# Seven gather buffers instead of eight, and a fourth kept unit of query weights, in a four-layer decoder trunk

## The chip, the core and the metric

The kernel runs on one core of a Trainium2 chip. The metric is the device time of one execution in microseconds (us); lower is better. Three executions of the kernel before took 3229.98, 3231.82 and 3232.85 us, so their median is 3231.82 us.

The core has five engines with instruction streams of their own: TensorE (PE, matrix products, with a separate weight load, PEld), VectorE (DVE), ScalarE (ACT), GpSimd (POOL) and SyncE (SP). They meet through semaphores. Sixteen DMA engines move data from device memory into the on-chip memory. Here POOL starts the gathers, and SP starts the plain loads of weights.

## The reference

The reference is a decoder trunk for one sequence of 256 tokens of width 1024, in float32. It has four layers. Each layer adds a token mixer and then a feed-forward part to the residual stream:

```python
for i in range(DEPTH):                       # DEPTH = 4
    h = h + mixer[i % 3](rmsnorm(h, norm_mix[i]), ...)      # HGRN2, FoX, Mamba-2 SSD, HGRN2
    h = h + peer_ffn(rmsnorm(h, norm_ffn[i]), peer_w_q[i], peer_keys[i], peer_u[i], peer_v[i])
return rmsnorm(h, norm_final)
```

The feed-forward part (PEER) is what fills the time. Each token forms 8 queries from a weight matrix of 1024 x 2048, scores two lists of 128 keys a query, keeps the best 16 of the 256 sums, and so names 16 experts a query. An expert is one row of `u` and one row of `v`, 1024 numbers each, out of a table of 16384 experts a layer:

```python
q = (xb @ w_q).reshape(M, 8, 2, 128)
...                                          # two top-16 lists, their sums, top 16 again: idx, gates
u, v = u_tab[idx], v_tab[idx]                # 128 experts of a token, 8 KB each
act = gelu(einsum('md,mhkd->mhk', xb, u)) * gates
return einsum('mhk,mhkd->md', act, v)
```

So 256 tokens x 128 experts x 4 layers x 8 KB have to come from device memory, beside the weights of the mixers and of the queries.

## The kernel before

**Stages.** The 256 tokens are two tiles of 128. A layer and a tile make a stage, eight in all (`STAGES`), in the order layer 0 tile 0, layer 0 tile 1, layer 1 tile 0, and so on. The main loop of a stage takes its 64 pairs of gathers. Beside them, as "side work", it runs the mixer, the normalisation and the queries of the *next* stage (`side`, `ready`, `queries`), so that the experts of the next stage are known when this one ends. The eighth stage has almost no side work. The loop spreads the side work by costs that are written out by hand (`SIDE`, `SPAN`, `products_`, `others`).

**Gathers.** One gather brings 128 rows of 8 KB, a `u` row and a `v` row together, into one buffer of 128 x 2048 numbers (1 MB): two experts of 64 tokens, as the token's number decides the partition. Two gathers are a pair, which serves two experts of all 128 tokens, so there are 512 pairs and 1024 gathers. The buffers `GB[0]` to `GB[NGB - 1]` form a ring, and gather n goes to buffer n modulo NGB. `fetches(i)`, called at the start of pair i, hands POOL all gathers below 2i + NGB whose experts are known. The work on a pair is in `dot` and `spread`. DVE multiplies the `u` half with the token (in place) and sums it up, one instruction a gather. ACT applies the activation and the gate, and spreads the result on a diagonal (`dg`). PE multiplies that with the `v` half into two accumulators (`acc`, L1257); four float32 products a pair are eight records in the profile. When the last of them is done the two buffers are free, and POOL, which waits for that (L1221), issues the next two gathers.

**Weights.** All weights come in units of 1 MB, in a fixed sequence (`stream`): the units of a layer's mixer, then its eight query units `wq`, for tile 0 and again for tile 1. `loads()` issues them from SP (L303) in the order of `order`, as long as a place is free. A unit's place is one of three:

- one of the `NRAW` = 3 rotating `raw` buffers, given free when PE has used the unit
- a place named in `homes`, only in the first stage, where the gather buffers and the mixer's memory still lie idle; these units need no `raw` buffer
- for the first `NKEPT` units of a layer's `wq`, a place in `kept`. It is loaded for tile 0 and not again for tile 1 of the same layer; such a unit needs no `raw` buffer either

`loads()` is called each time PE has used up a unit (`half`). Of the eight `wq` units of a layer, three are kept, so tile 1 loads five.

**Memory.** `kept`, the ring `gb` and the rest lie side by side in one tile, `arena`; a unit and a gather buffer have the same size.

**The end.** After the last gather, PE has to wait for DVE and ACT before the last pair's products. `warm` issues products on constants into a spare bank, with no use for their result; in the last pair there is one of them ahead of the products (L1239, float32, two records). Then the last normalisation runs on DVE and ACT, and the result is written.

Of the kernel before, what the change touches and what calls it, by code (L numbers as in the profile page):

```python
# [25 lines left out]
HALF = UNIT // 2  # L26
TOPK = 16
NQ = TOPK // 2
NGB = 8
NRAW = 3  # L30
MIX = 10464
STAGES = 2 * DEPTH
NKEPT = 3

FREE = {"hg": 0, "fox": 64 + 8 * T + 2 * D, "ssd": 352 + 4 * D + 96}
SPACE = 7 * D + P
# [128 lines left out]
def trunk(ctx: ExitStack, tc: tile.TileContext, d: dict, out: bass.AP):  # L165
# [12 lines left out]
    cst = cpool.tile([P, ncst], F32, name="cst")  # L178
    par = cpool.tile([P, npar], F32, name="par")
    fst = cpool.tile([P, P + 8 * 2 * DEPTH], F32, name="fst")  # L180
    sizes = (("h", 2 * D), ("xT", D), ("XR", 2 * D), ("keys", UNIT), ("SS", 2048), ("mix", MIX), ("kept", NKEPT * UNIT),
             ("gb", NGB * 2 * D))
    arena = cpool.tile([P, sum(n for _, n in sizes)], F32, name="arena")
# [8 lines left out]
    SS = at_["SS"].rearrange("p (h c k) -> p h c k", h=8, c=2)  # L192
    GB = [at_["gb"][:, i * 2 * D:(i + 1) * 2 * D] for i in range(NGB)]
    mix = at_["mix"]
# [17 lines left out]
    def act(o, i, f, **k):  # L212

        if f not in ghosts:
            table[0] = f
        nc.scalar.activation(o, i, f, **k)  # L216
# [36 lines left out]
    def bank():  # L253
        return psp.tile([P, 512], F32, name="ps")
# [7 lines left out]
            stream += [(nm, i) for i in range(UNITS[KIND[l] if KIND[l] != "ssd" else "ssm"])]  # L262
            stream += [("wq%d" % l, i) for i in range(8)]

    homes = {3: GB[0], 4: GB[1], 17: GB[0], 18: GB[1], 19: GB[2], 23: GB[5], 24: GB[6]}
    homes.update({28 + i: mix[:, o:o + UNIT] for i, o in enumerate((SPACE, D, 3 * D))})
    order = [0, 1, 2, "rest", *range(3, 9), 23, 9, 10, 11, 24, 12, 13, 14, 22, 15, 16, "x", 17, 20, 18, 21, 19, "keys",
             "factors", 28, 25, "heads", 29, 26, 27, "states", 30]
# [7 lines left out]
    def loads():  # L276

        while order:
# [11 lines left out]
            else:  # L290
                nm, i = stream[u]
                keep = nm[0] == "w" and i < NKEPT
                if keep:
# [925 lines left out]
    def fetch(n):  # L1219
        (s, hh, q), g = pairs[n // 2], n % 2  # L1220
        nc.gpsimd.indirect_dma_start(GB[n % NGB], None, d["uv"],  # L1221
                                     bass.IndirectOffsetOnAxis(ap=got[s, hh][0][:, g, q:q + 1], axis=0))

    def fetches(n):

        while sent[0] < 2 * len(pairs) and sent[0] < 2 * n + NGB and pairs[sent[0] // 2][:2] in got:
            fetch(sent[0])
            sent[0] += 1

    def dot(i, g):  # L1230
        if g == 0:
            acts[i] = wk2.tile([P, 3, 2], F32, name="dots", bufs=4)
        u = GB[(2 * i + g) % NGB][:, 0:D]
        stt(u, u, 1.0, XR[:, g], op0=OP.mult, op1=OP.mult, accum_out=acts[i][:, 0, g:g + 1])

    def warm(n, b, x):

        for _ in range(n):
            nc.tensor.matmul(b, x[:, 0:P], x[:, 0:512], start=True, stop=True)  # L1239

    def spread(i):
        s, hh, q = pairs[i]
        a = acts.pop(i)
        dg = wk2.tile([P, 2, 64], F32, name="dg", bufs=4)
        act(a[:, 1], a[:, 0], AF.Gelu)
        for g in range(2):
            act(a[:, 2, g:g + 1], a[:, 1, g:g + 1], AF.Copy, scale=got[s, hh][1][:, g, 1, q:q + 1])
        for g in range(2):
            act(dg[:, g], m64, AF.Copy, scale=a[:, 2, g:g + 1])
        if hh == 0 and q == 0:  # L1250
            accs[s] = [accp.tile([P, 512], F32, name="acc") for _ in range(2)]
        if i == len(pairs) - 1:
            warm(1, bank(), cst)
        for e in range(2):
            for g in range(2):
                v = GB[(2 * i + g) % NGB][:, D + e * 512:D + (e + 1) * 512]
                nc.tensor.matmul(accs[s][e][g * 64:g * 64 + 64], dg[:, g], v, start=hh == 0 and q == 0,  # L1257
                                 stop=hh == 7 and q == NQ - 1)
# [67 lines left out]
    for s in range(STAGES):  # L1326
# [23 lines left out]
        for i in range(64 * s, 64 * s + 64):  # L1350
            new, end = i % 64 == 0 and s > 0, i % 64 == 63 and s + 1 < STAGES
            fetches(i)
            dot(i, 0)
            if end:
                for o, b in x[:2]:
                    nc.scalar.copy(o, b)
            elif new:

                products_(True)
                others()  # L1360
            dot(i, 1)
            spread(i)
            if end:
                (_, b), (o, c) = x[2:]
                nc.scalar.copy(x[2][0], b)
                vec.tensor_copy(o, c)
            route_steps(3, i // 8 + 3)
            others()
            products_()
            if i % 64 == 62 and s + 1 < STAGES:  # L1370
                while not state["done"]:
                    others()
                    products_(True)
                others()
                x = repeated()
            if table[0] is not AF.Gelu:
                act(spare, eps, AF.Gelu)
# [20 lines left out]
```

## Time and profile before

| what | value |
|---|---|
| median of three executions | 3231.82 us |
| time of the profiled execution | 3228.44 us |
| its span, first to last instruction | 3225.7 us |
| PE busy | 2490.0 us (77%) |
| DVE busy | 2117.9 us (66%) |
| ACT busy | 1352.9 us (42%) |
| POOL busy | 1182.8 us (37%) |
| moved by DMA | 1322.99 MB, mean 410 GB/s |

The profiled execution is 3.4 us below the median of the others. Its span leaves out 2.7 us that lie around it. In the views, a group is named by its line, engine and tile (`arena<-in_uv,ix` is a gather into the ring, `acc<-arena,dg` a product of `v` rows). A wait is put down to the instruction or the DMA that ended last. A line of the timeline begins with the start in us and the length in us. In a table of stretches the last three columns are the granted TensorE clock as a share of full speed, the mean busy share of the 16 DMA engines and what they moved in GB/s; a share can read 1.01 since packets overlap a little.

### The profile page before, as it was taken

What the parts mean: (1) busy time and instruction counts of PE and PEld (TensorE: products, weight loads), DVE (VectorE), ACT (ScalarE), POOL (GpSimd) and SP (SyncE); (2) the same over time, 40 slices, a digit from 0 to 9 for tenths busy, and PEclk for the clock granted to TensorE, in tenths of its full rate; (3) what the DMA queues carried; (4) which work ended last, traced back from release to release, by engine and by line L of the source; (5) the groups of instructions that cost most, each with busy time, mean ns of one, the idle gap of its engine ahead of it and who ended that gap; (6) DMA issues with size and microseconds to landing.
All of it is one profiled execution on the core that took longest, in us unless ns stands there. A gap on an engine that the chain in (4) does not pass through costs nothing.

```text
span 3225.7 us, 30835 instructions
## 1 busy us (share of the span) xinstructions
PE 2490.0 (77%) x8606; PEld 1102.5 (34%) x8606; DVE 2117.9 (66%) x5584; ACT 1352.9 (42%) x3895; POOL 1182.8 (37%) x1030
## 2 busy tenths in 40 slices
PE   9888787777777886898778897878777788866565
PEld 4433233233333432344233443333323333332222
DVE  2476657566666866788567876576666667667764
ACT  3353334253334633477234673354433544333332
POOL 0243334333443443333334333343433343334443
PEclk9999898888899897999889998889988998888777
DMA  7899999999999999999999999999999999999997
GB/s 312 345 421 421 421 421 419 420 412 410 421 418 421 399 421 414 420 421 419 412 416 418 416 420 409 416 413 421 418 418 416 409 421 420 413 413 416 419 417 329
DMA packets 182761, 1322.99 MB, mean 410 GB/s; under 512 B 20289, under 2 KB 20673, under 8 KB 21825
## 3 DMA queue, kind: packets, MB, share of 16 engines
q0 software_dynamic: 147456, 1073.81, 80.6%
q1 hardware_dynamic: 35136, 247.23, 18.6%
q8 instruction: 71, 1.16, 0.1%
q14 instruction: 98, 0.79, 0.1%
HBM read 1319.90 MB, written 1.05 MB: 410 GB/s over the span
## 4 chain that ended last, share of the span: by engine, by line
DMA 56%; PE 18%; DVE 9%; issue 8%; ACT 5%; POOL 3%; POOLq 0%; SPq 0%; DVEq 0%; ACTq 0%
DMA arena<-in_uv,ix 56%; PE acc L1257 9%; DVE arena L203 7%; PE pj L238 6%; POOL arena L1221 3%; PE ps L238 3%; ACT dots L216 2%; ACT L216 1%; ACT dg L216 1%; PE ps L242 1%; ACT arena L216 1%; DVE si L203 0%; DVE eq L203 0%; DMA raw<-in_ssm 0%; DVE sv L203 0%
## 5 line engine op out<-in xcount | busy, mean ns | idle before, releaser
L1221 POOL DMA_INDIRECT arena<-in_uv,ix x1024 | 1180.7, 1153 | 2017.0 <-PE acc L1257 1475.8
L203 DVE SCALAR_TENSOR_TENSOR arena<-arena 128x1024 f32<-128x1024 f32 (+3 forms) x1282 | 1322.1, 1048 | 907.3 <-DMA arena<-in_uv,ix 848.5
L1257 PE MATMUL acc<-arena,dg 128*64 128x512 f32 x4096 | 1306.0, 723 | 712.8 <-ACT dg L216 697.9
L1257 PEld LDWEIGHTS acc<-arena,dg 128*64 128x64 f32 x4096 | 474.9, 154 | 1354.9 <-ACT dg L216 1021.5
L238 PE MATMUL pj<-raw,arena 128*128 128x512 f32 x1648 | 772.5, 611 | 3.7 <-DMA raw<-in_ssm 1.6
L216 ACT ACTIVATE dots<-dots 128x2 f32<-128x2 f32 x512 | 103.6, 202 | 1531.6 <-DVE arena L203 1529.2
L238 PEld LDWEIGHTS pj<-raw,arena 128*128 128x128 f32 x1648 | 301.4, 193 | 482.2 <-issue 470.6
L216 ACT ACT_TABLE_LOAD x325 | 417.0, 1283 | 6.8 <-DVE arena L203 0.8
L216 ACT ACTIVATE dg<-m,dots 128x64 f32<-128x64 f32 x1024 | 292.5, 333 | 0.0
L216 ACT ACTIVATE dots<-dots,gs 128x1 f32<-128x1 f32 x1024 | 245.6, 286 | 16.7
L238 PE MATMUL ps<-arena 128*128 128x128 f32 (+3 forms) x992 | 130.2, 288 | 1.3 <-ACT arena L1087 0.9
L238 PEld LDWEIGHTS ps<-arena 128*128 128x128 f32 (+2 forms) x992 | 103.0, 168 | 67.8 <-issue 43.2
L238 PE MATMUL pj<-arena 128*128 128x512 f32 (+1 forms) x288 | 125.8, 584 | 0.3 <-DVE arena L203 0.3
L242 PEld LDWEIGHTS ps<-fst,arena 128*128 128x128 f32 x568 | 68.5, 148 | 88.9 <-issue 42.7
L242 PE MATMUL ps<-fst,arena 128*128 128x128 f32 x568 | 92.8, 291 | 7.7 <-DVE arena L203 5.0
L216 ACT ACTIVATE arena<-arena 128x512 f32<-128x512 f32 (+3 forms) x132 | 67.7, 554 | 43.3 <-DVE arena L203 40.9
L203 DVE DVE_READ_ACCUMULATOR arena<-arena 128x1 f32 x1024 | 83.9, 82 | 0.0
L238 PEld LDWEIGHTS pj<-arena 128*128 128x128 f32 x288 | 53.0, 192 | 71.4 <-issue 61.7
L203 DVE FIND_INDEX8 si<-sv,arena 128x8 uint32<-128x128 f32 x256 | 69.8, 284 | 0.0
L203 DVE MAX8 sv<-arena 128x8 f32<-128x128 f32 x256 | 61.7, 282 | 10.3 <-ACT arena L1091 5.7
L238 PE MATMUL ps<-cst,arena 128*128 128x128 f32 (+3 forms) x288 | 68.0, 364 | 0.0
L203 DVE COPY gs<-ig 64x16 f32<-64x16 f32 (+1 forms) x256 | 51.8, 202 | 4.7
(116 smaller groups left out, 1232.6 us busy)
## 6 DMA issues: line engine op xcount, KB each, us to landing
raw<-in_hg SPq DMA_DIRECT2D x72, 1024.0 KB
raw<-in_ssm SPq DMA_DIRECT2D x64, 1024.0 KB
raw<-in_wq SPq DMA_DIRECT2D x38, 1024.0 KB
raw<-in_fox SPq DMA_DIRECT2D x32, 1024.0 KB
arena<-in_uv,ix POOLq DMA_INDIRECT x1024
arena<-in_wq SPq DMA_DIRECT2D x14, 1024.0 KB
arena<-in_hg SPq DMA_DIRECT2D x8, 1024.0 KB
arena<-in_keys SPq DMA_DIRECT2D x4, 1024.0 KB
```

The source lines that it names most:

```text
L203: return getattr(nc.vector, name)(o, *a, **k)
L216: nc.scalar.activation(o, i, f, **k)
L238: nc.tensor.matmul(o, w, m, start=start, stop=stop)
L242: nc.tensor.transpose(o, i, ident)
L1221: nc.gpsimd.indirect_dma_start(GB[n % NGB], None, d["uv"], bass.IndirectOffsetOnAxis(ap=got[s, hh][0][:, g, q:q + 1], axis=0))
L1257: nc.tensor.matmul(accs[s][e][g * 64:g * 64 + 64], dg[:, g], v, start=hh == 0 and q == 0, stop=hh == 7 and q == NQ - 1)
```

## The change

The ring has seven buffers. Its eighth megabyte goes to `kept`, which now holds four units: the units 0 to 3 of each layer's `wq` are loaded for tile 0 and stay for tile 1. The size of `arena` stays the same, and all buffers of the ring begin one place further on.

In the first stage, unit 23 of the stream (the fourth query unit of layer 0) was loaded to `GB[5]` and unit 24 to `GB[6]`. Unit 23 now goes to its place in `kept`, and unit 24 to `GB[5]`. The order of the loads is unchanged.

In the last pair, `warm` issues two products on constants instead of one.

```diff
-NGB = 8
+NGB = 7
...
-NKEPT = 3
+NKEPT = 4
...
-    homes = {3: GB[0], 4: GB[1], 17: GB[0], 18: GB[1], 19: GB[2], 23: GB[5], 24: GB[6]}
+    homes = {3: GB[0], 4: GB[1], 17: GB[0], 18: GB[1], 19: GB[2], 24: GB[5]}
...
         if i == len(pairs) - 1:
-            warm(1, bank(), cst)
+            warm(2, bank(), cst)
```

## The prediction

> **What bounds the kernel now.** I read the page first: the DMA queues, the rate by slices and the chain of work that ended last.
>
> ```profile
> PE 2490.0 (77%) x8606; PEld 1102.5 (34%) x8606; DVE 2117.9 (66%) x5584; ACT 1352.9 (42%) x3895; POOL 1182.8 (37%) x1030
> ...
> GB/s 312 345 421 421 421 421 419 420 412 410 421 418 421 399 421 414 420 421 419 412 416 418 416 420 409 416 413 421 418 418 416 409 421 420 413 413 416 419 417 329
> ...
> q0 software_dynamic: 147456, 1073.81, 80.6%
> q1 hardware_dynamic: 35136, 247.23, 18.6%
> ...
> DMA 56%; PE 18%; DVE 9%; issue 8%; ACT 5%; POOL 3%; POOLq 0%; SPq 0%; DVEq 0%; ACTq 0%
> ```
>
> Between the first two slices and the last one the rate never leaves 399 to 421 GB/s, and 421 comes again and again: that is a ceiling. No compute engine is near its own. The gathers (q0) are four fifths of the traffic, the weights (q1) the rest. The chain is DMA for 56% only, and that speaks for another bound: a ring that turns too slowly. So I next asked for stretches (length, busy time of the engines, then clock, DMA share, GB/s) and for the longest waits.
>
> ```profile
> 150.00:516.00 366.00, 289.33 (x1001) 124.69 (x999) 243.02 (x637) 150.66 (x433) 138.78 (x122) 0.90 1.01 421
> 516.00:3200.00 2684.00, 2049.69 (x7059) 900.70 (x7061) 1814.31 (x4786) 1146.63 (x3338) 1028.89 (x891) 0.89 1.01 416
> 150.00:3200.00 3050.00, 2339.02 (x8060) 1025.38 (x8060) 2057.32 (x5422) 1297.30 (x3771) 1167.66 (x1012) 0.89 1.01 417
> ```
>
> ```profile
> POOL arena L1221 <- PE acc L1257: 1475.8, 439, 8.9
> ...
> DVE arena L203 <- DMA arena<-in_uv,ix: 848.5, 548, 5.1
> ```
>
> POOL waits 1475.8 us for PE to free a buffer. In a closed ring with a saturated server that is what is expected: whoever feeds the server waits. The question is whether the DMA engines ever wait for POOL. They lose (421 - 417) / 421 of 3050 us, about 29 us, against the ceiling. This is the room in which a shorter ring can hurt.
>
> How much is in the queue? I compared the first gather, which finds nothing ahead of it, with the gather that, past the first twenty, has the shortest time from its POOL row to its DVE product (n-th gather row with n-th product row), and with the last one, of a stretch without weights.
>
> ```profile
> 118.15 1.08 POOL L1221 DMA_INDIRECT arena<-in_uv,ix  x1 [116.46 <-DVE ig L203]
> ...
> 123.84 1.23 DVE L203 SCALAR_TENSOR_TENSOR arena<-arena 128x1024 f32<-128x1024 f32 x1 [5.13 <-DMA arena<-in_uv,ix]
> ...
> 2901.57 0.94 POOL L1221 DMA_INDIRECT arena<-in_uv,ix  x1 [2.86 <-PE acc L1257]
> ...
> 2910.99 1.23 DVE L203 SCALAR_TENSOR_TENSOR arena<-arena 128x1024 f32<-128x1024 f32 x1 [0.19 <-DMA arena<-in_uv,ix]
> ...
> 3199.45 0.94 POOL L1221 DMA_INDIRECT arena<-in_uv,ix  x1 [0.30 <-issue]
> ...
> 3212.00 1.23 DVE L203 SCALAR_TENSOR_TENSOR arena<-arena 128x1024 f32<-128x1024 f32 x1 [1.15 <-DMA arena<-in_uv,ix]
> ```
>
> Alone: 5.69 us. The last: 12.55 us, so 6.9 us of it is queue. The tightest one (the 905th): 9.42 us, still 3.7 us of queue. So the bytes bound the kernel, and the ring covers its own latency.
>
> **Part 1: four loads less.** Each layer's second tile loads five query units, and each first tile all eight.
>
> ```profile
> raw<-in_wq SPq DMA_DIRECT2D x38, 1024.0 KB
> ...
> arena<-in_wq SPq DMA_DIRECT2D x14, 1024.0 KB
> ```
>
> ```profile
> 363.00 73.50 SPq L303 DMA_DIRECT2D raw<-in_wq  x5
> ...
> 699.74 1.39 SPq L303 DMA_DIRECT2D arena<-in_wq  x3
> 718.05 92.43 SPq L303 DMA_DIRECT2D raw<-in_wq  x5
> ```
>
> 38 + 14 = 52 = 4 x (8 + 5). The first of these rows is a second tile (layer 0), the other two a first tile (layer 1). With four kept it is 4 x (8 + 4) = 48. Four loads of 1024 KB are 4.19 MB: 9.96 us at 421 GB/s, 10.06 us at the 417 of the whole body. I take **-10.0 us**. All of it lies where the DMA is the server that everything waits for, since the loads sit in the stretches of the rows above. The Trainium skill ("DMA: Bandwidth & Descriptors", section "Where 436 GB/s comes from") says that for transfers from HBM to SBUF the HBM side binds, at about 358 GB/s a core; by that a load would cost 2.93 us, the four 11.7 us, and the time would come out 1.7 us lower. The rows of 421 GB/s contradict it for this kernel, and the measurement decides.
>
> On SP four issues fall away and nothing waits for them. In first tiles the fourth unit goes out right behind the third (as the three of the row at 699.74 do) and no longer waits for a `raw` buffer; the same bytes come earlier. Each `raw` buffer then runs one unit further ahead: cost 0, covered by the loads' own lead.
>
> **Part 2: seven gathers in the ring.** In each turn POOL issues two gathers when a pair is done. Now the total issued by then is one less, so a gather has one transfer less ahead of it: 1.05 MB / 421 GB/s = 2.49 us. The tightest gather keeps 9.42 - 2.49 = 6.93 us, 1.2 us over the 5.69 of a gather alone; the last one 10.06. No gather of the steady turn would find the DMA empty.
>
> A second way to see it is the loop. Without weights three pairs take 6 x 2.49 = 14.9 us. With seven buffers the first gather issued at the end of pair n is the second one of pair n + 3. It needs 5.69 us alone, then the end game of the pair: in the rows below, from the product at 3212.00 to the block at 3214.28, 2.28 us, and the block itself, 2.17 to 3.77 us. Together 10.1 to 11.7 us against 14.9. So 3.2 to 4.8 us of delay in one turn are still absorbed. Before, the pair issued at the end of pair n was pair n + 4: four pairs, 19.9 us, against 12.6 to 14.2 us (one transfer more to land), a slack of 5.7 to 7.3.
>
> The disturbances are there, however. This is one of the moments behind the dips of the slices:
>
> ```profile
> 1062.70:1065.20 2.50, 2.50 (x18) 1.67 (x18) 2.02 (x5) 1.10 (x3) 1.92 (x2) 0.75 0.71 233
> ```
>
> For 2.5 us the engines are busy to 71% only, so some of the 16 have run dry already with eight buffers. Lower bound of the cost: 0, since a buffer less cannot make a gather start sooner. Upper bound: the shortfall of 29 us doubles. I take **+1.0 us**, because the nearest row is the tightest gather, and it stays above 5.69.
>
> In the first turn the new homes matter.
>
> ```profile
> 127.29 0.93 POOL L1221 DMA_INDIRECT arena<-in_uv,ix  x1 [3.10 <-PE pj L238]
> ...
> 130.73 1.29 POOL L1221 DMA_INDIRECT arena<-in_uv,ix  x1 [2.50 <-PE pj L238]
> ...
> 132.32 0.94 POOL L1221 DMA_INDIRECT arena<-in_uv,ix  x1 [0.30 <-issue]
> ...
> 136.09 0.94 POOL L1221 DMA_INDIRECT arena<-in_uv,ix  x1 [2.83 <-PE acc L1257]
> ...
> 137.34 1.24 DVE L203 SCALAR_TENSOR_TENSOR arena<-arena 128x1024 f32<-128x1024 f32 x1 [1.14 <-DMA arena<-in_uv,ix]
> ...
> 143.69 1.22 DVE L203 SCALAR_TENSOR_TENSOR arena<-arena 128x1024 f32<-128x1024 f32 x1 [1.19 <-DMA arena<-in_uv,ix]
> ```
>
> The sixth gather waits at 127.29 for unit 23 and the seventh at 130.73 for unit 24. Now the sixth waits for unit 24, until 130.73; alone it would land by 136.4, and its product starts at 137.34. The eighth (132.32) now waits for pair 0, until 136.09; alone it would land by 141.8, its product starts at 143.69. Cost 0, covered by the gathers ahead.
>
> **Part 3: a second product on constants.**
>
> ```profile
> 3209.32 2.17 PE L1257 MATMUL acc<-arena,dg 128*64 128x512 f32 x8 [1.35 <-ACT dg L216]
> 3211.41 1.13 PE L1239 MATMUL ps<-cst 128*128 128x512 f32 x2
> 3214.28 3.77 PE L1257 MATMUL acc<-arena,dg 128*64 128x512 f32 x8 [1.73 <-ACT dg L216]
> ```
>
> ```profile
> 3209.32:3211.50 2.18, 2.18 (x9) 1.01 (x9) 1.23 (x2) 0.18 (x1) 0.00 (x0) 1.00 0.06 26
> ...
> 3214.28:3218.05 3.77, 3.77 (x8) 1.44 (x8) 1.38 (x2) 0.98 (x4) 0.00 (x0) 0.55 0.00 0
> ```
>
> One such product takes at most 1.13 us, and PE stands idle for 1.73 us before the last block, so the second one fits: cost 0. The last block ran at a granted clock of 0.55 and took 3.77 us; the one before, at 1.00, 2.17. If the shorter idle time keeps the clock up, the end comes up to 1.60 us sooner, less what DVE needs for the first half of the last addition. I bound it by 0 and -1.6 and take **-0.5 us**, as nothing shows whether the unprofiled runs met the low clock there.
>
> **Sum.** -10.0 + 1.0 - 0.5 = -9.5 us. The profiled execution took 3228.44 us (span 3225.7, 2.7 around it), so it would take 3218.9. The median of the runs lies 3.4 us above that execution: 3231.82 - 9.5 = **3222.3 us**, 0.29% less. A change under 0.2%, 6.5 us, can hardly be told from none here.
>
> **Rivals.**
>
> - *The shorter ring gives part of it back.* The queue runs dry in the dips that are there already, for 4 to 16 us more. For it: the dips, and a margin of 1.2 us at the tightest gather. Against it: the typical gather keeps over 4 us of queue. Time: 3231.8 - 10.0 - 0.5 + 10 = 3231.3, within 0.2%. Chance 0.25.
> - *The shorter ring costs more than the loads.* One mechanism: each dip deepens because every turn of the ring starts with 2.49 us less work queued, so the shortfall of 29 us doubles, at the end of pairs whose work PE and DVE do late. It decides against the change from 10 us of new shortfall on, a third of the present one; in the view of stretches the body would then fall below about 415.6 GB/s. Time: 3231.8 - 10.0 + 29 - 0.5 = 3250. For it: POOL's 439 waits and a chain that is DMA for only 56%. Against it: 421 flat from 150 to 516 us with the same ring. Chance 0.12. Beside it stands the Trainium skill, same page, section "Why a DMA increments its semaphore by 16 and not by 1": the engines of one transfer finish independently, and only the last of 16 tells that the data has landed. By that rule the engines that are ahead must find their next packet in the ring, and a shorter one makes them stop more often.
> - *The four loads were hidden anyway*, and the ring's turn sets the pace: 3231.8 + 1.0 - 0.5 = 3232.3. Against it: the gather at 12.55 us waits 6.9 us in a queue. It shares the 0.25 of the first rival, as the time is the same.
>
> **How the numbers follow.** The forecast, 0.63, has a range of its own of 3219 to 3226. Faster by over 0.2% needs less than 3225.4: a ring cost of up to 4 us. That holds 0.62; same 0.26; slower 0.12. The range for 8 in 10 goes from 3218.5 (no ring cost, all of part 3) to 3236, into the rivals of a small loss; it leaves out most of the slow rival.
>
> **What would show it.** `in_wq` loads: 31 into `raw` and 17 into `arena`; q1 at 243.04 MB. The body's rate stays at 416 to 418 GB/s, and the time from gather to product falls by about 2.5 to 3 us (the last one near 10). Right on part 3: two products on constants at the end and a last block of 2.2 us. Wrong, if the rate of the body falls below 415.6, with new waits of DVE on gathers that had nothing ahead of them, 5.7 to 6.5 us after their issue.

## The result and the profile after

Twenty runs of the changed kernel have a median of 3225.95 us (3222.33 to 3233.07), twenty runs of the kernel before beside them 3231.41 us (3229.5 to 3233.7). The ratio is 0.9986, with a 95% interval of 0.9979 to 0.9992: 4.5 us less (2.6 to 6.8). It isn't formed from the two medians, which lie 5.5 us apart. The gain is there, but it is below the 0.2% (6.5 us) that the prediction set as its bound, and only about half of the 9.5 us that it forecast. The profiled execution happens to be the slowest of the twenty: 3233.07 us, span 3231.2. So its rows can show mechanisms, but its length must not be set against the profile before. For that, the experiments below bring other profiles of rings of seven. Of all executions below, one of 7544.09 us, with seven buffers alone, is left out of its ratio.

The page of the changed kernel: the rate by slices, the hardware queue, the chain that ended last, and the loads of query units.

```profile
GB/s 316 332 416 421 421 396 411 421 421 411 413 420 421 410 406 414 417 421 421 413 407 420 420 412 407 402 406 421 420 419 415 406 421 420 390 414 420 418 419 350
...
q1 hardware_dynamic: 34560, 243.03, 18.2%
...
DMA 47%; PE 20%; DVE 12%; issue 12%; ACT 5%; POOL 4%; POOLq 0%; SPq 0%; DVEq 0%; ACTq 0%
...
raw<-in_wq SPq DMA_DIRECT2D x31, 1024.0 KB
arena<-in_wq SPq DMA_DIRECT2D x17, 1024.0 KB
```

31 + 17 = 48 loads: four fewer, as meant, and 4.2 MB less on the queue. But the slices dip more often (396, 406, 402, 390), and the chain is DMA for 47%, where it was 56%: more of the chain now runs through PE, DVE and the issue of gathers. The same stretches as before:

```profile
150.00:516.00 366.00, 292.64 (x992) 123.86 (x992) 243.19 (x640) 150.83 (x433) 137.05 (x122) 0.89 1.01 415
516.00:3200.00 2684.00, 2043.96 (x7064) 900.59 (x7060) 1811.74 (x4783) 1147.12 (x3335) 1017.14 (x889) 0.89 1.01 414
150.00:3200.00 3050.00, 2336.60 (x8051) 1024.46 (x8049) 2054.93 (x5423) 1297.95 (x3767) 1154.19 (x1011) 0.89 1.01 414
```

The stretch from 150 to 516 us, flat at 421 before, has fallen to 415; the body from 417 to 414. In time, 421 to 414 is 1.7% of 3050 us, some 51 us, against 29. In the other profiles of the changed ring it is milder, as will be seen.

The totals of two of the longest waits have hardly moved, and they would not have told this:

```profile
POOL arena L1221 <- PE acc L1257: 1434.3, 418, 9.1
DVE arena L203 <- DMA arena<-in_uv,ix: 857.2, 537, 5.0
```

The single gathers do tell it. As in the prediction, the n-th gather row is set beside the n-th product row. This is the timeline of the changed kernel: three gathers (the 136th, the 392nd, the last), each with the DVE product that waits for it.

```profile
526.24 0.94 POOL L1221 DMA_INDIRECT arena<-in_uv,ix  x1 [3.98 <-DVE si L203]
...
532.52 1.23 DVE L203 SCALAR_TENSOR_TENSOR arena<-arena 128x1024 f32<-128x1024 f32 x1 [0.93 <-DMA arena<-in_uv,ix]
...
1287.70 1.07 POOL L1221 DMA_INDIRECT arena<-in_uv,ix  x1 [4.13 <-PE acc L1257]
...
1293.68 1.23 DVE L203 SCALAR_TENSOR_TENSOR arena<-arena 128x1024 f32<-128x1024 f32 x1 [0.83 <-DMA arena<-in_uv,ix]
...
3209.78 1.14 POOL L1221 DMA_INDIRECT arena<-in_uv,ix  x1 [2.58 <-PE acc L1257]
...
3219.10 1.23 DVE L203 SCALAR_TENSOR_TENSOR arena<-arena 128x1024 f32<-128x1024 f32 x1 [1.50 <-DMA arena<-in_uv,ix]
```

They take 6.28, 5.97 and 9.32 us from issue to product. A gather alone takes 5.69, so the first two found next to nothing ahead of them. The same 136th gather in the timeline of the kernel before:

```profile
517.21 1.78 POOL L1221 DMA_INDIRECT arena<-in_uv,ix  x1 [0.30 <-issue]
...
530.18 1.23 DVE L203 SCALAR_TENSOR_TENSOR arena<-arena 128x1024 f32<-128x1024 f32 x1 [1.14 <-DMA arena<-in_uv,ix]
```

It took 12.97 us. So this gather has lost 6.7 us of queue, and not the 2.49 us of one transfer. Two tables of stretches show what the DMA engines did around it, first the changed kernel, then the kernel before at the same gathers (share of the DMA engines and GB/s are the last two columns).

```profile
522.00:524.00 2.00, 1.51 (x4) 0.94 (x6) 2.00 (x10) 0.68 (x4) 0.26 (x1) 0.68 1.04 422
524.00:526.20 2.20, 2.20 (x6) 0.46 (x2) 2.17 (x11) 0.96 (x5) 0.00 (x0) 0.51 0.93 365
526.20:528.70 2.50, 2.18 (x9) 0.93 (x8) 2.50 (x5) 1.43 (x5) 2.10 (x2) 1.00 0.80 295
```

```profile
520.00:522.50 2.50, 1.41 (x7) 0.37 (x3) 2.50 (x9) 0.52 (x3) 1.06 (x1) 1.00 1.02 413
522.50:525.00 2.50, 2.04 (x8) 0.93 (x8) 1.99 (x7) 1.87 (x7) 1.39 (x2) 1.00 1.01 406
```

The changed kernel drops to 365 and 295 GB/s with the engines busy to 93% and 80%; the kernel before stays above 400. What held the ring up is in the timeline of the changed kernel just ahead of the 136th gather:

```profile
521.37 0.48 DVE L203 MAX8 sv<-arena 128x8 f32<-128x128 f32 x2
...
522.49 5.89 PE L1257 MATMUL acc<-arena,dg 128*64 128x512 f32 x16 [2.91 <-ACT dg L216]
...
525.09 0.48 DVE L203 MAX8 sv<-arena 128x8 f32<-128x128 f32 x2
```

This is a place where DVE searches the next stage's top 16 between its products, and where PE works on the blocks of two pairs for 5.89 us without a break, with a granted clock of 0.51 from 524.00 to 526.20. The buffers come free late, POOL waits 3.98 us (the row puts the end of this wait down to the search, which ended within 0.3 us of the first of the two blocks), and next to nothing is left in the queue. The kernel before has the same search at this place, with one gather more in hand, and its two blocks take 2.17 us each at a granted clock of 1.00.

So two things meet here, the shorter ring and a slow block. The seven profiles of rings of seven tell them apart to some degree. Where the granted clock was 1.00 in the 4 us ahead of the issue, the 136th gather took 8.02 and 10.41 us; where it was 0.50 to 0.69, in the other five, 5.90 to 7.77. In all six profiles of rings of eight the clock was 1.00 there, and the gather took 11.84 to 14.64 us. A ring of eight with a slow block at this place isn't among the traces.

The end, from the timeline of the changed kernel (two products on constants, then the last block):

```profile
3219.65 1.98 PE L1239 MATMUL ps<-cst 128*128 128x512 f32 x4
...
3221.56 1.98 PE L1257 MATMUL acc<-arena,dg 128*64 128x512 f32 x8
```

The last block takes 1.98 us instead of 3.77. Whether the second product did that is taken up below.

### The profile page after: what moved, and what is told of

It is laid out like the page before. It is cut to its first block, busy times and chain, and to the rows that moved or that the text cites. A ratio compares the mean times of both kernels' runs of the same rounds, so it can differ in the third digit from the quotient of the medians.

```text
span 3231.2 us, 30846 instructions
## 1 busy us (share of the span) xinstructions
PE 2492.9 (77%) x8608; PEld 1103.6 (34%) x8608; DVE 2116.5 (66%) x5584; ACT 1354.0 (42%) x3895; POOL 1173.3 (36%) x1030
## 3 DMA queue, kind: packets, MB, share of 16 engines
q1 hardware_dynamic: 34560, 243.03, 18.2%
## 4 chain that ended last, share of the span: by engine, by line
DMA 47%; PE 20%; DVE 12%; issue 12%; ACT 5%; POOL 4%; POOLq 0%; SPq 0%; DVEq 0%; ACTq 0%
DMA arena<-in_uv,ix 47%; PE acc L1257 11%; DVE arena L203 9%; PE pj L238 6%; POOL arena L1221 4%; PE ps L238 2%; ACT dots L216 2%; ACT L216 1%; ACT dg L216 1%; PE ps L242 1%; DVE eq L203 0%; ACT arena L216 0%; DVE si L203 0%; DVE sv L203 0%; DVE af L203 0%
## 5 line engine op out<-in xcount | busy, mean ns | idle before, releaser
L238 PE MATMUL pj<-raw,arena 128*128 128x512 f32 x1592 | 750.9, 614 | 3.7 <-DMA raw<-in_ssm 2.4
L238 PEld LDWEIGHTS pj<-raw,arena 128*128 128x128 f32 x1592 | 293.2, 195 | 469.3 <-issue 451.6
L238 PE MATMUL pj<-arena 128*128 128x512 f32 (+1 forms) x344 | 152.0, 588 | 0.3 <-DVE arena L203 0.3
L238 PEld LDWEIGHTS pj<-arena 128*128 128x128 f32 x344 | 63.4, 193 | 88.0 <-issue 78.3
L203 DVE MAX8 sv<-arena 128x8 f32<-128x128 f32 x256 | 61.7, 283 | 11.3 <-ACT arena L1091 5.7
```

What stands on the lines that cost most here:

```text
L203: return getattr(nc.vector, name)(o, *a, **k)
L238: nc.tensor.matmul(o, w, m, start=start, stop=stop)
```

## The experiments

The theory that entered them: the loads are worth their bytes, the ring costs about 1 us, the second product on constants about half a microsecond. The rival: the ring gives back several microseconds. Each ran beside the kernel before, and the ratio is against that; the two times given are medians, and the ratio isn't formed from these.

**The ring alone.** Only the ring is shortened. Nothing takes the place of the eighth buffer.

```diff
-NGB = 8
+NGB = 7
```

> The kernel before with seven buffers in the ring and nothing else changed (three kept units, one product on constants). Theory A, the change is a sum of two terms that both reach the end: the four loads are worth the full 10 us and the shorter ring costs 4 to 6 us. Then this one takes 3231.4 + 5 = about 3236 us (3234 to 3239). Theory B, the loads were half hidden and the ring costs nothing: 3231.4 us, within 1 us of the kernel before.

3229.36 us against 3228.29, ratio 1.0004 (0.9995 to 1.0013). A second measurement, on another chip:

> Seven buffers alone once more, since 1.3 us with 3 us to either side left open whether the ring costs 1 or 5 us. If the changed kernel's missing gain is the ring's, 4 to 6 us above the kernel before; if it lies in something else of the change, 0 to 2 us.

3229.14 against 3227.61, ratio 1.0007 (0.9998 to 1.0016). The ring alone costs 1.3 and 2.3 us, neither of them clear of nothing. The term of +1.0 stands, for a kernel with all its loads; the 4 to 6 us that the other theory asked for didn't come. Yet the profile of the first of these has gathers already that found nothing ahead of them (its 882nd, in the timeline), and the rate of the body has hardly changed:

```profile
2847.30 0.94 POOL L1221 DMA_INDIRECT arena<-in_uv,ix  x1 [3.59 <-PE acc L1257]
...
2852.98 1.23 DVE L203 SCALAR_TENSOR_TENSOR arena<-arena 128x1024 f32<-128x1024 f32 x1 [1.32 <-DMA arena<-in_uv,ix]
```

```profile
150.00:3190.00 3040.00, 2331.96 (x8041) 1025.26 (x8039) 2051.57 (x5413) 1294.64 (x3759) 1152.43 (x1008) 0.89 1.01 416
```

5.68 us, the time of a gather that is alone. The price of the ring can't be read from its tightest gather, neither way.

**The loads alone.** The ring keeps eight buffers, and the fourth query unit isn't loaded a second time. As there is no memory for it, second tiles read the third unit's place in its stead: the same work on a wrong unit of weights.

```diff
-                keep = nm[0] == "w" and i < NKEPT
+                skip = nm[0] == "w" and i == NKEPT and (nm, i) in seen
+                keep = nm[0] == "w" and i < NKEPT or skip
...
-                    r = at_["kept"][:, i * UNIT:(i + 1) * UNIT]
+                    j = min(i, NKEPT - 1)
+                    r = at_["kept"][:, j * UNIT:(j + 1) * UNIT]
+                    if skip:
+                        kept.add((nm, i))
...
+                seen.add((nm, i))
```

> The kernel before, eight buffers, with exactly four loads less: the fourth query unit of a layer's second tile is read from the place of the third, so 512 of the 2048 query columns of the second tiles come from wrong weights (48 loads of query units in all). Theory A, a load is worth its transfer: 9.96 us below the kernel before (8.5 to 11.5). Theory B, the loads are half hidden: 5 us below.

3217.54 against 3228.61, ratio 0.9966 (0.9954 to 0.9978): -11 us (-7 to -15). The page counts the loads, and a stretch gives the rate of the body:

```profile
raw<-in_wq SPq DMA_DIRECT2D x34, 1024.0 KB, 13.4
...
arena<-in_wq SPq DMA_DIRECT2D x14, 1024.0 KB, 16.5
```

```profile
150.00:3190.00 3040.00, 2333.57 (x8062) 1026.13 (x8060) 2056.24 (x5421) 1298.22 (x3772) 1164.44 (x1012) 0.89 1.01 417
```

48 loads, and the rate of before: the whole price of four transfers shows in the time. A first form of this experiment had noted a unit as seen when its load was first tried, not when it was issued, and so left out seven loads (31 + 14 = 45), three of them in first tiles, which then also read the third's place.

```diff
+                seen.add((nm, i))
                 keep = nm[0] == "w" and i < NKEPT or skip
```

> The kernel before, eight buffers, with the four loads left out and no memory spent on it: the fourth query unit of a layer's second tile is read from the place of the third, so the second tile's queries are computed from wrong weights for 512 of their 2048 columns. The number of instructions is the same but for the four loads. Theory A: 3231.4 - 10 = about 3221.4 us (3220 to 3223). Theory B, loads half hidden: about 3226.5 us.

3209.11 against 3228.29, ratio 0.9938 (0.9925 to 0.9952): -20 us (-15 to -24). The experiment missed its four, but it gives a second price: 2.9 us a load (2.2 to 3.5). With a ring of eight, bytes are time.

**The second product on constants alone.**

```diff
-            warm(1, bank(), cst)
+            warm(2, bank(), cst)
```

> The kernel before with two products on constants ahead of the last pair instead of one, nothing else. Both theories: 0 to -1 us (3230.4 to 3231.4), and in the profile a last block of about 2.0 to 2.2 us instead of 3.8, with under 1 us of idle time ahead of it. If the last block was fast in most runs of the kernel before as well, the median doesn't move.

3228.71 against 3228.29, ratio 1.0000 (0.9991 to 1.0009). Its timeline at the end:

```profile
3214.71 1.98 PE L1239 MATMUL ps<-cst 128*128 128x512 f32 x4
...
3217.56 2.17 PE L1257 MATMUL acc<-arena,dg 128*64 128x512 f32 x8 [0.86 <-ACT dg L216]
```

The last block ran in 2.17 us after 0.86 us of idle time, as forecast. But so it did without the second product. All five other profiles of kernels that have one product there show a last block of 2.17 us. This is the end of one of them, the first form of the loads-alone kernel above, with the longest idle time of the five:

```profile
3193.36 1.13 PE L1245 MATMUL ps<-cst 128*128 128x512 f32 x2
...
3196.18 2.17 PE L1263 MATMUL acc<-arena,dg 128*64 128x512 f32 x8 [1.69 <-ACT dg L216]
```

So the 3.77 us of the profile before were one case in six, and the short block can't be put down to the second product. Nor is it always free: from the product of the last gather to the last block it is 2.27 or 2.28 us with one product, and in six of the eight profiles with two 2.46 to 3.01: there the products on constants start late, behind a block of 3.48 to 3.86 us, and PE is not yet through with them.

**The changed kernel with six buffers**, to see how steep the price of the ring is.

```diff
-NGB = 7
+NGB = 6
```

> The changed kernel with one buffer less again: six in the ring, four kept units, two products on constants. If a buffer costs what it takes from the queue (a threshold: the pair issued at the end of pair n is then needed three pairs later with two transfers to land, 12.6 to 14.2 us of latency against 14.9 us of transfers), it loses far more than the step from eight to seven: 15 to 50 us above the changed kernel, 3241 to 3276 us. If each buffer costs the same 5 us: about 3231 us.

3326.46 against 3228.29, ratio 1.0309 (1.0295 to 1.0323): +100 us. A stretch and its waits:

```profile
150.00:3190.00 3040.00, 2305.57 (x7915) 1013.50 (x7915) 2012.76 (x5330) 1275.75 (x3679) 1118.96 (x976) 0.89 1.00 404
```

```profile
DVE arena L203 <- DMA arena<-in_uv,ix: 962.4, 613, 5.3
```

The body falls to 404 GB/s, and DVE waits over 100 us longer for gathers. One buffer costs 1 to 2 us from eight to seven with all loads, the next one, with 48 loads, about 100: seven sits just ahead of the bend.

**The changed kernel again**, with two variants on the same chip. In the second, unit 24 goes back to its former home; in the third, PE moreover finishes one buffer of a pair ahead of the other, except in the last pair. That was meant to free the first buffer sooner.

> The changed kernel once more, on the chip of the other runs of this call. If the loads give 10 us, the ring costs 1 us (as seven buffers alone did) and nothing else happens, it is 9 us below the kernel before. If the new homes of the first stage cost 2.5 us, as the sixth gather's product at 139.89 us in the profile of the changed kernel against 137.34 before says, it is 6 to 7 us below. By the first measurement of it, 4.5 us below.

```diff
-    homes = {3: GB[0], 4: GB[1], 17: GB[0], 18: GB[1], 19: GB[2], 24: GB[5]}
+    homes = {3: GB[0], 4: GB[1], 17: GB[0], 18: GB[1], 19: GB[2], 24: GB[6]}
```

> The changed kernel with unit 24 of the first stage loaded to the last buffer of the ring, GB[6], instead of GB[5], so that the sixth gather has its buffer at once and the seventh waits for unit 24 as it did in the kernel before. If the homes cost what the first turn shows: 2 to 3 us below the changed kernel, and the sixth gather's product back at about 137 us. If the first turn's delay is made up later by the ring: no difference.

```diff
-        for e in range(2):
-            for g in range(2):
+        eg = [(e, g) for e in range(2) for g in range(2)]
+        if i < len(pairs) - 1:
+            eg.sort(key=lambda x: x[1])
+        for e, g in eg:
```

> As the changed kernel with unit 24 in GB[6], and besides the order of the four products of a pair is turned (both halves of the first gather's rows, then both of the second's; the last pair keeps its order), so that the first buffer of a pair is free after half the block, 1.0 to 1.9 us sooner. If the cost of seven buffers is latency of the ring, 1 to 3 us below the kernel with unit 24 in GB[6]; if that cost is only 1 us, no difference beyond 1 us.

| kernel | median, us | ratio to before (3228.61 us) |
|---|---|---|
| changed kernel | 3223.30 | 0.9982 (0.9973 to 0.9991) |
| with the former home | 3222.98 | 0.9989 (0.9979 to 0.9998) |
| with the order of the products too | 3223.63 | 0.9984 (0.9975 to 0.9993) |
| loads alone, ring of eight (from above) | 3217.54 | 0.9966 (0.9954 to 0.9978) |

The first three can't be told apart. So the new home of unit 24 shows no cost, as forecast, though one of 2 us would not be seen. The order of the products tells nothing, as it didn't free a buffer sooner. POOL still issued at the end of the block, here 939.03 us, and not at its half:

```profile
936.86 2.17 PE L1259 MATMUL acc<-arena,dg 128*64 128x512 f32 x8 [1.64 <-ACT dg L216]
...
939.06 0.93 POOL L1221 DMA_INDIRECT arena<-in_uv,ix  x1 [5.26 <-PE acc L1259]
```

Over the gathers that waited so, the issue came 0.04 us (median) after the last product of the block in this kernel, and in the changed kernel as well: in both traces the semaphore that POOL waits for is raised with the block's last product. So it stays open what it is worth to free a pair's buffers one by one. Against the last row of the table 5 to 6 us are missing. The stretch of the changed kernel beside these runs is nearer to the kernel before than that of its slowest run was:

```profile
150.00:3190.00 3040.00, 2333.73 (x8050) 1025.42 (x8048) 2053.95 (x5417) 1295.46 (x3763) 1161.99 (x1010) 0.89 1.01 416
```

**Seven buffers and the skipped loads, without kept units.** The loads-alone kernel with `NGB = 7`: three kept units, the old homes, no early load of a fourth unit, no second product on constants; second tiles again read the third's place. What it has in common with the changed kernel is the ring and the 48 loads.

```diff
-NGB = 8
+NGB = 7
```

> Seven buffers in the ring and exactly four loads less, but without the fourth kept place: the fourth query unit of a second tile is read from the place of the third (wrong weights for 512 of 2048 query columns there), all first tiles load as in the kernel before, and the homes and the end are those of before. If the loads' 11 us and the ring's cost simply add and the ring costs 1 us, 10 us below the kernel before. If it stands at 5 to 6 us below, like the changed kernel, the ring's cost is about 5 us once the loads are gone, and neither the new homes nor the fourth kept unit's early load has a part in it.

3225.49 against 3227.61, ratio 0.9991 (0.9982 to 1.0000): -2.9 us. It does as the changed kernel does, within the noise, so neither the place of the kept unit nor its early load nor the end is needed to take the gain away. The ring of seven does it, and only together with fewer loads:

| ratio to before | 52 loads | 48 loads |
|---|---|---|
| ring of eight | 1 | 0.9966 |
| ring of seven | 1.0004, 1.0007 | 0.9991; changed kernel 0.9986, 0.9982 |

Of the four loads, the ring of eight turns some 11 us into time; by the difference in the lower row, from +1.8 to between -2.9 and -5.8, the ring of seven turns 5 to 8 of them into time. The means are enough for the sign: with four loads at 11.3 us (from both loads-alone kernels, +-2.1), the ring at 1.8 (+-2.1) and the five kernels with a ring of seven and 48 loads at -4.4 (+-1.3), the part that doesn't add up is 11.3 - 1.8 - 4.4 = 5.1 us, and 2 to 8 with these intervals taken as independent.

**Two weight buffers instead of a gather buffer**, to find a version that keeps both: ring of eight, four kept units, `NRAW` = 2, three more units of the first stage at home in the idle ring.

```diff
-NGB = 7
-NRAW = 3
+NGB = 8
+NRAW = 2
...
-    homes = {3: GB[0], 4: GB[1], 17: GB[0], 18: GB[1], 19: GB[2], 24: GB[5]}
+    homes = {2: GB[3], 5: GB[6], 8: GB[7], 3: GB[0], 4: GB[1], 17: GB[0], 18: GB[1], 19: GB[2], 24: GB[5]}
```

> The fourth kept unit paid with another buffer: the ring keeps eight, the weights rotate in two buffers instead of three (three units of the first stage get free gather buffers as homes, so that the start keeps its lead). If two weight buffers are enough, the kernel keeps the loads' gain without the ring's cost: about 11 us below the kernel before, 3217 to 3219 us. If PE then waits for weights in the dense mixers, slower than the changed kernel, with waits of the products on raw in place of the 3 us that stand there now.

3228.37 against 3227.61, ratio 1.0005 (0.9996 to 1.0014): none of the 11 us. Its stretches and the largest two of its new waits:

```profile
0.00:150.00 150.00, 136.80 (x506) 71.04 (x508) 48.63 (x142) 45.31 (x93) 14.11 (x17) 0.99 0.75 297
150.00:3190.00 3040.00, 2328.47 (x8056) 1016.25 (x8054) 2054.41 (x5417) 1301.15 (x3770) 1163.98 (x1009) 0.89 1.01 417
```

```profile
PEld pj L238 <- DMA raw<-in_ssm: 32.6, 18, 4.2
PE pj L238 <- DMA raw<-in_ssm: 23.2, 15, 3.3
```

The body is back at 417 GB/s with 48 loads. PE now waits for weights, without harm to that rate. By the profile, the fastest of this kernel's eleven executions, most of the gain goes in the start, where the kernel before moves 322 GB/s:

```profile
0.00:150.00 150.00, 138.81 (x516) 72.55 (x517) 49.95 (x144) 48.29 (x101) 14.78 (x19) 0.99 0.80 322
```

25 GB/s over 150 us are 3.75 MB, at most 8.9 us at 421 GB/s. The product of the 17th gather starts at 179.5 us here and at 173.8 in the kernel before, 5.7 us late. An attempt to win them back gave the three idle gather buffers to nine units of the first stage, in turn:

```diff
-    homes = {2: GB[3], 5: GB[6], 8: GB[7], 3: GB[0], 4: GB[1], 17: GB[0], 18: GB[1], 19: GB[2], 24: GB[5]}
+    homes = {2: GB[3], 5: GB[6], 6: GB[7], 9: GB[3], 10: GB[6], 11: GB[7], 14: GB[3], 15: GB[6], 16: GB[7], 3: GB[0], 4: GB[1], 17: GB[0], 18: GB[1], 19: GB[2], 24: GB[5]}
```

> As the kernel with eight gathers, four kept units and two rotating weight buffers, but nine units of the first stage (2, 5, 6, 9, 10, 11, 14, 15, 16) use three idle gather buffers in turn as homes, so that the start has a lead of five units. In the profile of that kernel the first 150 us moved 297 GB/s against 322 before, which is 25 / 421 of 150 us, about 9 us, and the body's rate was that of before. If the start was what ate the loads' gain: 10 to 11 us below the kernel before, 3217 to 3219 us, below both kernels, with 318 to 323 GB/s in the first 150 us. If two weight buffers cost it in the body, by waits of the products on raw: no better than the kernel before.

3260.31 against 3227.30, ratio 1.0100 (1.0083 to 1.0117). A miss of the edit: a home that is used twice gets its second unit before the first one's products, so that the first mixer partly works on other units' weights, and the loads queue up behind one another.

```profile
0.00:150.00 150.00, 114.50 (x427) 60.90 (x428) 31.85 (x88) 37.43 (x70) 1.16 (x5) 0.90 0.56 226
```

96 GB/s less over 150 us are 34 us, about the loss of 33. It says nothing on two weight buffers with a start as full as before. No version that beats the changed kernel by what these runs can tell was found.

## Why the prediction was partly right

The time of 3225.95 us lies inside the range, 3.7 us above the forecast of 3222.3, and the gain of 0.14% (0.08 to 0.21) falls to the case "within 0.2%", which had 0.26. The case that the forecast stood for, faster by over 0.2%, had 0.62.

- *Four loads less, -10.0:* right in a ring of eight, where they gave -11 (-7 to -15), and seven gave -20. The runs alone couldn't tell 2.49 us a load from 2.93, but the rows of 421 GB/s, here as before, speak for 2.49. The 2.93 is the estimate by the 358 GB/s of the Trainium skill ("DMA: Bandwidth & Descriptors", section "Where 436 GB/s comes from"), which the section gets by halving a stack's 716 GB/s between two cores; it names 425 GB/s, measured on a transfer of 16 MB, beside it.
- *The second product on constants, -0.5:* the short block came, but not by the cause that was forecast, as five profiles with one product have it too. The term was drawn from one profile that happened to have a slow last block; the time shows nothing (1.0000 +- 0.0009), which allows 0 as well as -0.5. Its cost of 0, as "the second one fits", held in two of eight profiles.
- *New homes, 0:* not refuted. The product of the sixth gather came at 139.89 and 139.34 us in the two profiles of the changed kernel, 2.0 to 2.6 us later than told, but the kernel with the former home is no faster.
- *The ring, +1.0:* this is the mis-sized term. Alone it measured +1.3 and +2.3, but with the four loads gone the ring of seven takes about 6.6 us (-11.0 with eight, -4.4 with seven). The sum put terms together that don't add up: that each was nearly right alone, and the sum still in its range, is partly luck.

The step behind it that failed is "so a gather has one transfer less ahead of it: 2.49 us", from which "No gather of the steady turn would find the DMA empty" was drawn. A shorter ring doesn't take one transfer from each gather. A pair frees two buffers together. With eight, the two gathers issued then are those of one pair. With seven, they are the second gather of one pair and the first of the next. So the first gather of a pair is issued on the same event as before, and the second waits for one pair more, about two transfers. Over all gathers past the first twenty, in the profiles before and after, the first of a pair went from 15.5 to 14.0 us, median from issue to product, and the second from 16.6 to 12.0. That is 1.5 and 4.6 us where the forecast had 2.5 for each. The gather that the argument took as the tightest, the 905th, is a first one. The shortest after are second ones: the 136th (12.97 to 6.28 us), the 392nd (11.97 to 5.97), the 882nd (11.33 to 6.16). The tightest turn of the old ring wasn't the tightest of the new one. The loop that the prediction sets beside this step does name the two gathers rightly; the delay of 3.2 to 4.8 us that it leaves for a turn was used up where they took 5.68 to 6.28 us.

This step alone doesn't give the loss, since the ring of seven with 52 loads has the same times from issue to product (14.1 and 12.0 us). Why the moments in which the queue is dry cost little with 52 loads and more with 48 is argued, not shown. The time lost against the ceiling, from the packets of each trace between 150 and 3190 us against 421.5 GB/s, goes with it:

| kernel | lost, us |
|---|---|
| ring of eight (52, 52, 48, 48 and 45 loads) | 33.7, 36.7, 34.6, 34.3, 34.5 |
| ring of seven, 52 loads | 36.7, 36.1 |
| ring of seven, 48 loads | 51.2 (slowest run), 43.2, 37.7, 42.9, 41.4 |
| ring of six, 48 loads | 126 |

A likely reason: a weight load doesn't depend on the ring. While POOL waits for buffers, a load that stands in its own queue keeps the engines busy, and its bytes have to be moved anyway. With fewer of them some dry moments have nothing to fill them. (The kernel with nine homes isn't in the table, as its gathers begin only at 151 us.)

Where the extra loss lies fits this. Split each trace into stages, from the product of a stage's first gather to that of the next, the first stage from its 17th. Four stages prepare a second tile, and these have lost a load each. With seven buffers they lose 19 and 20 us together with 52 loads, and 24 to 31 with 48. The three that prepare a first tile, with eight loads as ever, lose 15 and 16 us, and then 10 to 18. With eight buffers the four lose 17 and 20 us with 52 loads, and 18 to 23 with 48 or 45. The extra loss is where the loads are missing. Single traces differ by several us, though, so this supports the reason and doesn't prove it. A ring of seven with far fewer loads would test it; it wasn't tried.

Of the rivals, the first (the ring gives back 4 to 16 us) comes nearest: 6.6 us of ring where it took 10 beyond the loads, so that its time of 3231.3 us is 5 us too long. The second, the shortfall doubling and a time of 3250 us, didn't come; with six buffers the loss went from 34 to 126 us. The Trainium skill says ("DMA: Bandwidth & Descriptors", section "Why a DMA increments its semaphore by 16 and not by 1") that the engines of one transfer finish independently. The landings agree: of the gathers for which a trace has all 16 increments of the semaphore, one from each engine, the last came 3.3 us (median) after the one before it in the kernel before, and 0.8 us in the changed kernel. So part of what the prediction took for queue, 6.9 us at the last gather, can be the wait for one late engine. No run here separates engines that stop early from pairs that are simply late. That the loads were hidden anyway is refuted by the loads alone.

The signs that the prediction named came out as follows: 31 + 17 loads and 243.03 MB, the time from gather to product down by about 3 us (last one 12.55 to 9.32), two products and a short last block, all as told. The sign that it had named for being wrong came too: in the changed kernel's slowest run the body was at 414 GB/s, with gathers at 5.97 and 6.28 us, and in its other profile at 415.5, just below the bound of 415.6, with gathers at 5.92 and 6.20.

## What to carry to other kernels

The price of a buffer and the price of a transfer need not add up when both act on the same saturated queue: before trading one for the other, measure each alone and then both, in four cells. When a ring whose buffers come free in groups gets an odd length, work out per slot which event issues it; here half of the slots lost nearly two transfers of lead, not one. The typical queue and the tightest moment of the old ring both said little about the new one here, and the bend was one buffer away (1 to 2 us, then 100). And before a slow block in one profile is given a remedy, look for it in other profiles.

## What the runs showed of the hardware that was not expected

The times of some kernels with a ring of seven scatter more: the twenty runs after spread over 10.7 us, the twenty before over 4.2; the kernel with the former home spread over 10.9 us in eleven runs, the ring of seven with skipped loads over 9.5. But the changed kernel's other eleven runs spread over 5.1 us, where the kernel before spread over 5.9 beside them. So it isn't shown that the ring does it.

The idle time ahead of a block doesn't tell its length by itself. In the timeline of the kernel before, a block of eight records took 2.17 us at 519.24 us after 3.29 us of idle time, and another 3.60 us at 527.48 after 2.35.

The waits of PE and of its weight loads for units still on the way, some 110 us when both are added up (they wait partly at the same time) with two weight buffers, where the kernel before has about 3, left the body's rate at 417 GB/s.
